# Attention scores of two directions, summed on VectorE before the product with the values, in a hybrid attention and expert block

## The chip, the cores and the metric

One core of one Trainium2 chip runs the kernel. The metric is the device time of one execution in microseconds (us). Engines: TensorE (PE: matmuls, and PEld, its weight loads), VectorE (DVE), ScalarE (ACT), GpSimd (POOL) and SyncE (SP, which here issues the large loads). Each engine runs its own instructions in order, and waits for another engine or a transfer at the places that the build has set.

## The reference, cut to what matters

One layer on 256 tokens of width 1024, with 256 context tokens ahead of them. A combined projection feeds two branches: a gated linear attention that runs over the tokens forward and backward (8 heads of 128, chunks of 64), and a chunk MLP. Both are projected, gated, added and projected again; a top-4-of-32 mixture of experts follows. The part that the change touches, for one direction:

```python
scores = jnp.einsum('bthd,bshd->bhts', qc * jnp.exp(b - b_ref), kc * jnp.exp(b_ref - b))
scores = jnp.where(lower, scores, 0.0)
o = (jnp.einsum('bhts,bshv->bthv', scores, vc)
     + jnp.einsum('bthd,bhdv->bthv', qc * jnp.exp(b), s))
...
o = (gla_chunked(q, k_f, i, logf_f, s_fwd0)
     + rev(gla_chunked(rev(q), rev(k_b), rev(i), rev(logf_b), s_bwd0)))
```

The output of a head is the sum of both directions, and the values (`i`) are the same in both.

## The kernel before

The kernel has a prefix (modulation, projection, attention, MLP branch, branch and output projections, router) and an expert part that streams the weights of 32 experts, 2 MB at a time, through a ring of buffers.

The projection's large products run as split fp32: `parts` (L316, through `split` at L258 and L259) writes a weight granule as a rounded `ghi` (on ACT, L258) and a rest `glo` (on DVE, L259), and `dense` (L325 to L340) makes three matmuls for each block, all recorded as L339. A granule of 256 columns is loaded by L311, 1 MB, on SP's queue.

Attention is done in pairs of heads, five turns `j` = 0 to 4. In turn `j` the projections of pair `j` (`d` steps) are written in between the steps of the two heads of pair `j`-1 (`x` and `y`: 0 `decays`, 1 `states`, 2 `output`, 3 `finish`) and two modulation steps (`m`), by a list written by hand:

```python
ORDER = "x0 d0 y0 m0 d1 x1 m1 d2 x2 y1 x3 m2 d3 y2 m3 y3 d4"
```

The four steps of a head:

- `decays` (L436 to L471): logarithms on ACT (L443), cumulative sums by scans on DVE (L450), differences `d1` (L459), exponentials on ACT (L462 to L466), products on DVE (L468 to L470). L469 and L470 end it; `e1`, `e2` lie in the tile `lf`.
- `states`: scores of both directions into PSUM (L487, 32 small matmuls), masked into one of two tiles `masked` (L490, named `attc` in the trace), keys transposed (L497) and copied (L498), outer products of keys and values (L506, L509).
- `output`: the chunk states are chained on DVE (L520, L521); then, into `o_ps`, scores times values (L525) and queries times states (L529).
- `finish`: the norm of the head. `rstd_of` is a chain of some twelve small DVE operations (L105 to L111, about 0.2 us apart), `on` scales (L543), PE transposes `on` (L546), `y` multiplies the gate in (L548), and a split writes it into `yhl`.

Behind the last turn come: the projection of `v` in four granules, each followed by `prefetch` (L623: the first three 2 MB pieces of expert 0, into buffers that lie where attention's tiles lay); the norm of `v` (L638 to L643); branch_a, four granules of `w_branch_a` times `yhl` (L339 `acc<-yhl`); then the MLP branch, where L657 multiplies `v` by a position matrix into `o_ps` and L660 evicts it. L684 is 8 small matmuls for the router's base.

The build decides the order of each engine's instructions: it schedules by its own estimate of times, and keeps the written order only in part. So an edit can move rows far from it. The expert part has an order written by hand.

Of the kernel before, what the change touches and what calls it, by code (L numbers as in the profile page):

```python
# [26 lines left out]
def view(t, off, dims):  # L27
    return bass.AP(tensor=t.tensor, offset=t.offset + off, ap=[t.ap[0], *dims])
# [3 lines left out]
def kernel(  # L32
# [5 lines left out]
    ve, sc, te, gp = nc.vector, nc.scalar, nc.tensor, nc.gpsimd  # L38
# [122 lines left out]
    for h in range(2):  # L161
        b = slice(h * 64, h * 64 + 64)
# [16 lines left out]
    def bank(name, shape=(P, 2, T)):  # L179
        return ps.tile(list(shape), F32, name=name, bufs=2 if name in ("acc", "tp") else 1)  # L180
# [141 lines left out]
    def win(sec, j, pieces=False):  # L322
        return Granule(w_in[0, :, sec * D + j * 256:sec * D + (j + 1) * 256], pieces)
# [23 lines left out]
    def four_outs(pps, natural):  # L347
        if natural:
# [9 lines left out]
    start = [(win(1, 0, True), True, [bank("acc"), bank("acc")]), (win(2, 0, True), False, [bank("ua"), bank("ub")]),  # L358
             (win(3, 0, True), False, [bank("scores"), bank("o_ps")])]
# [23 lines left out]
    for k in range(2):  # L383
        a, b = cols2[:, 8 + 16 * k:16 + 16 * k], cols2[:, 16 + 16 * k:24 + 16 * k]
# [51 lines left out]
    def decays(hd, k, q):  # L436


        col = slice(hd, hd + 1)
        lf = wk.tile([P, 2, 2 * T], F32, name="lf")  # L440
        tc.keep_in_program_order(sc.preload_act_table_set("natural_log_exp_and_others"))
        for dr in range(2):
            tc.keep_in_program_order(sc.activation(lf[:, dr], k[:, dr], AF.Ln, scale=omlb[dr][:, col], bias=lb[dr][:, col]))  # L443
        kl, kc = k[:, :, 0:T], k[:, :, T:2 * T]
        bl = wk.tile([P, 2, T], F32, name="bl")
        cu = wk.tile([P, 2, T], F32, name="cu")
        ve.memset(view(cu, T - 1, [[1, 2]]), 0.0)

        def scan(dst, o, src, so, m, n, st):
            ve.tensor_tensor_scan(view(dst, o, [[st, n]]), m, view(src, so, [[st, n]]), 0.0, op0=OP.mult, op1=OP.add)  # L450

        whole = view(reset, 1, [[0, T - 1]])
        scan(bl, 0, lf, 0, reset, T, 1)
        scan(bl, 2 * T - 1, lf, 3 * T - 1, reset, T, -1)
        scan(cu, T - 2, lf, 2 * T - 1, whole, T - 1, -1)
        scan(cu, T + 1, lf, 3 * T, whole, T - 1, 1)
        e1, e2 = lf[:, :, 0:T], lf[:, :, T:2 * T]
        d1 = wk.tile([P, 2, T], F32, name="d1")
        ve.tensor_sub(view(d1, 0, [[T, 2], [64, 4], [1, 64]]), view(bl, 0, [[T, 2], [64, 4], [1, 64]]),  # L459
                      view(bl, 31, [[T + 1, 2], [64, 4], [0, 64]]))  # L460
        w = wk.tile([P, 2, 2, 4], F32, name="w")
        sc.activation(e1, d1, AF.Exp)  # L462
        sc.activation(e2, d1, AF.Exp, scale=-1.0)
        sc.activation(cu, cu, AF.Exp)
        sc.activation(w[:, 0], view(bl, 31, [[T + 1, 2], [64, 4]]), AF.Exp)
        sc.activation(w[:, 1], view(d1, 63, [[T - 63, 2], [64, 4]]), AF.Exp)  # L466
        for dr in range(2):
            ve.scalar_tensor_tensor(e1[:, dr], e1[:, dr], nomlb[dr][:, col], q, op0=OP.mult, op1=OP.mult)  # L468
        ve.scalar_tensor_tensor(e2, kl, -1.0, e2, op0=OP.add, op1=OP.mult)  # L469
        ve.scalar_tensor_tensor(cu, kc, -1.0, cu, op0=OP.add, op1=OP.mult)  # L470
        return e1, e2, cu, w  # L471

    def attend(hd, dec, iv, og):

        hh = hd % 2
        vs = slice(hh * P, hh * P + P)
        st = {}

        def states():
            qt, kt_, kc, w = dec  # L480
            for dr in range(2):
                for tt in range(2):
                    for b in range(4):
                        t0, n = 64 * (b // 2), 64
                        if b % 2 != dr:
                            t0, n = t0 + 32 * (1 - dr), 32
                        te.matmul(pst[32 * b:32 * b + 32, dr, tt, t0:t0 + n], kt_[:, dr, tt * P + 32 * b:tt * P + 32 * b + 32],  # L487
                                  qt[:, dr, tt * P + t0:tt * P + t0 + n], start=True, stop=True, skip_group_check=True)
            sm = masked[hd % 2]
            ve.copy_predicated(sm, view(mask, 0, [[P, 2], [0, 2], [1, P]]), pst)  # L490
            ks = consts.tile([P, 2, 2, 4, P], F32, name="ks", tag="big3")
            kn, S = ks[:, 0], ks[:, 1]
            for a, src in ((0, kt_), (1, kc)):
                pt = bank("tp", (P, 2, 2, P))
                for dr in range(2):
                    for tt in range(2):
                        te.transpose(pt[:, dr, tt], src[:, dr, tt * P:tt * P + P], ident)  # L497
                nc.any.tensor_copy(kn[:, a], pt.rearrange("p a b c -> p (a b) c"))  # L498
            ua = bank("ua", (P, 4, P))
            ub = bank("ub", (P, 4, P))  # L500
            U = {}
            for slot, even, odd in ((0, (0, 0), (0, 1)), (1, (0, 2), (1, 1)), (2, (1, 2), (1, 3))):
                for bk, (dr, ch) in ((ua, even), (ub, odd)):
                    s = slice((ch % 2) * 64, (ch % 2) * 64 + 64)
                    U[dr, ch] = bk[:, slot]
                    te.matmul(bk[:, slot], kn[s, 0, 2 * dr + ch // 2], iv[s, ch // 2, vs], start=True, stop=True)  # L506
            for bk, dr in ((ua, 0), (ub, 1)):
                for tt in range(2):
                    te.matmul(bk[:, 3], kn[:, 1, 2 * dr + tt], iv[:, 2 + tt, vs], start=tt == 0, stop=tt == 1)  # L509
            st.update(sm=sm, S=S, R=kn, U=U, ua=ua, ub=ub)  # L510

        def output():
            qt, w = dec[0], dec[3]
            sm, S, R, U, ua, ub = (st[k] for k in ("sm", "S", "R", "U", "ua", "ub"))
            sc.activation(S[:, 0, 0], ua[:, 3], AF.Copy, scale=w[:, 0, 0, 0:1])
            sc.activation(S[:, 1, 3], ub[:, 3], AF.Copy, scale=w[:, 0, 1, 3:4])
            for n in range(3):
                for dr, a, b in ((0, n, n + 1), (1, 3 - n, 2 - n)):
                    r = R[:, dr, b]
                    ve.tensor_add(r, S[:, dr, a], U[dr, a])  # L520
                    ve.tensor_scalar(S[:, dr, b], r, w[:, 1, dr, a:a + 1], w[:, 0, dr, b:b + 1], op0=OP.mult, op1=OP.mult)  # L521
            o = bank("o_ps", (P, 2, P))
            for tt in range(2):
                for dr in range(2):
                    te.matmul(o[:, tt], sm[:, dr, tt], iv[:, tt, vs], start=dr == 0, stop=False, skip_group_check=True)  # L525
                for dr in range(2):
                    for cc in range(2):
                        ch = 2 * tt + cc
                        te.matmul(o[cc * 64:cc * 64 + 64, tt], qt[:, dr, ch * 64:ch * 64 + 64], S[:, dr, ch],  # L529
                                  start=False, stop=dr == 1, skip_group_check=True)  # L530
            st["o"] = o

        def finish():
            o = st["o"]
            ss = sm2.tile([P, 2], F32, name="ss")
            for tt in range(2):
                junk = mid.tile([P, P], F32, name="junk2")
                sc.activation(junk, o[:, tt], AF.Square, accum_out=ss[:, tt:tt + 1])
            rs = sm2.tile([P, 2], F32, name="rs")
            rstd_of(rs, ss, 1.0 / P, sm2)  # L540
            on = wk.tile([P, 2, P], F32, name="on")
            for tt in range(2):
                ve.tensor_scalar(on[:, tt], o[:, tt], rs[:, tt:tt + 1], None, op0=OP.mult)  # L543
            pt = bank("tp", (P, T))
            for tt in range(2):
                te.transpose(pt[:, tt * P:tt * P + P], on[:, tt], ident)  # L546
            y = wk.tile([P, T], F32, name="y")
            ve.scalar_tensor_tensor(y, pt, gncol, og[:, hh], op0=OP.mult, op1=OP.mult)  # L548
            split(y, yhi[:, hd], ylo[:, hd])
        return states, output, finish  # L550

    sc2 = late.tile([P, 8], F32, name="sc2")
# [4 lines left out]
    for j in range(5):  # L557
        if j < 4:
            iv = wk.tile([P, 4, 256], F32, name="iv")
# [8 lines left out]
        if prev:  # L568
            piv, pq, pog, psg = prev
            heads = []  # L570
            for hh in range(2):
                dec = []
# [61 lines left out]
    st = late.tile([P, 2, 2, 6], F32, name="st")  # L634
# [15 lines left out]
    for j in range(4):  # L650
# [4 lines left out]
        for gg in range(2):  # L655
            for n in range(2):
                te.matmul(pss[:, gg, n], v[:, n, (2 * j + gg) * P:(2 * j + gg + 1) * P], wsT[:, 2 * j + gg],  # L657
                          start=True, stop=True)
# [43 lines left out]
    for j in range(4):  # L702
# [29 lines left out]
        for k in range(2):  # L732
            kt = 2 * j + k
            for tt in range(2):
                te.matmul(pl[:, tt], h2[:, k, tt * P:(tt + 1) * P], wr_sb[:, kt], start=kt == 0 and tt == 0,
                          stop=kt == KT - 1, skip_group_check=True)
# [353 lines left out]
```

## Time and profile before

| | |
|---|---|
| median of 3 runs | 1410.64 us (1410.29 to 1414.01) |
| profiled execution, its own time | 1409.58 us |
| its span | 1407.8 us |
| PE busy | 1335.7 us (95%) |
| DVE busy | 598.0 us (42%) |
| ACT busy | 302.0 us (21%) |
| moved by DMA | 487.35 MB, mean 346 GB/s |
| mean granted clock of PE | 0.988 |

The busy shares are means over the whole span. The two parts of the program have different limits, so that a stretch has to be read with its own row: PE's busy time, and the rate of the DMA engines.

### The profile page before, as it was taken

Reading aid. Unit: us, or ns where it says so; the run is one execution under the profiler, and the core shown is the slowest. Engines: PE = TensorE matmul, PEld = TensorE weight load, DVE = VectorE, ACT = ScalarE, POOL = GpSimd, SP = SyncE. Lnnn points to the kernel's source line nnn. Section 1 sums busy time; section 2 is a strip of 40 time slices with the busy share of each in tenths; the row PEclk is TensorE's granted clock in tenths of the full one; section 3 lists DMA queues with packets and bytes.
Section 4 is the critical chain, followed back from the end, with each engine's and each line's share of the span. In section 5 each row is a group of like instructions: output and inputs, shape, how many; then the busy total and the mean of one; then the engine's idle time right before and its main releaser. Section 6 shows DMA issues by size and latency. Waiting matters only on the chain. (4 is left out here: it accounts for less than half of the span.)

```text
span 1407.8 us, 18376 instructions
## 1 busy us (share of the span) xinstructions
PE 1335.7 (95%) x7815; PEld 722.9 (51%) x7815; DVE 598.0 (42%) x1176; ACT 302.0 (21%) x496; POOL 57.8 (4%) x59
## 2 busy tenths in 40 slices
PE   6999999989999999999999998989999899898986
PEld 4897988879999533333333332323323233232322
DVE  5578868697578322322232232222222222222214
ACT  3373645544344110000010010100001000010001
POOL 3000000000055000000000000000000000000001
PEclk7999999999999999999999999999999999999999
DMA  9545445366677989999999999999999999999995
GB/s 334 184 156 194 136 165 180 118 212 258 222 232 251 412 350 428 427 426 428 426 428 427 425 429 426 427 426 427 427 427 426 428 427 427 428 425 427 427 425 200
DMA packets 101264, 487.35 MB, mean 346 GB/s; under 512 B 5653, under 2 KB 64154, under 8 KB 76474
## 3 DMA queue, kind: packets, MB, share of 16 engines
q1 hardware_dynamic: 100042, 482.85, 85.3%
q0 software_dynamic: 848, 2.75, 0.7%
q8 instruction: 63, 1.03, 0.3%
q10 hardware_dynamic: 288, 0.52, 0.1%
q14 instruction: 23, 0.19, 0.0%
HBM read 485.06 MB, written 1.05 MB: 345 GB/s over the span
## 5 line engine op out<-in xcount | busy, mean ns | idle before, releaser
L828 PE MATMUL gate<-w,xT 128*64 128x512 f32 x1024 | 271.2, 608 | 18.3 <-DMA w<-in_w_dram 17.2
L828 PE MATMUL lin<-w,xT 128*64 128x512 f32 x1024 | 263.9, 594 | 0.0
L865 PE MATMUL py<-w,hT 128*64 128x512 f32 x992 | 221.0, 594 | 18.0 <-DMA w<-in_w_dram 18.0
L884 DVE SCALAR_TENSOR_TENSOR acc<-sc,wts,acc 128x512 f32<-128x512 f32 x122 | 86.0, 746 | 208.9 <-PE sc L881 208.9
L828 PEld LDWEIGHTS lin<-w,xT 128*64 128x64 f32 x1024 | 73.5, 137 | 147.8 <-issue 147.8
L339 PE MATMUL acc<-hh,glo 128*128 128x256 f32 (+1 forms) x480 | 146.2, 305 | 2.5 <-DVE glo L259 2.5
L339 PE MATMUL acc<-hh,ghi 128*128 128x256 f32 (+1 forms) x480 | 147.5, 307 | 0.7 <-ACT iv L424 0.7
L865 PEld LDWEIGHTS py<-w,hT 128*64 128x64 f32 x992 | 70.1, 136 | 149.2 <-issue 114.1
L259 DVE TENSOR_TENSOR glo<-w,ghi 128x1024 fp32r<-128x1024 f32 (+1 forms) x99 | 125.6, 1276 | 48.9 <-ACT ghi L258 48.7
L339 PE MATMUL acc<-hl,ghi 128*128 128x256 f32 (+1 forms) x480 | 145.1, 302 | 0.0
L828 PEld LDWEIGHTS gate<-w,xT 128*64 128x64 f32 x1024 | 62.0, 136 | 159.6 <-issue 96.0
L258 ACT ACTIVATE ghi<-w 128x1024 fp32r<-128x1024 f32 (+1 forms) x102 | 101.4, 1009 | 141.7 <-PE acc L339 68.3
L868 DVE TENSOR_TENSOR y<-py,g2h 128x512 f32<-128x512 f32 x31 | 21.4, 692 | 177.9 <-PE py L865 177.9
L339 PEld LDWEIGHTS acc<-hh,glo 128*128 128x128 f32 x480 | 90.0, 188 | 8.3 <-DVE glo L259 3.7
L339 PEld LDWEIGHTS acc<-hh,ghi 128*128 128x128 f32 x480 | 90.3, 188 | 5.3 <-ACT iv L424 0.9
L339 PEld LDWEIGHTS acc<-hl,ghi 128*128 128x128 f32 x480 | 90.3, 188 | 3.8 <-issue 0.4
L803 ACT ACTIVATE xT<-misc,sh,a 128x128 f32<-128x128 f32 (+1 forms) x68 | 30.7, 451 | 282.1 <-DVE xT L805 282.1
L805 DVE TENSOR_SCALAR xT<-misc,a,sh 128x128 f32<-128x128 f32 (+1 forms) x68 | 27.2, 401 | 138.3 <-PE misc L799 127.8
L836 ACT ACTIVATE s<-g 128x512 f32<-128x512 f32 x32 | 20.2, 630 | 288.3 <-DVE g L835 288.3
L799 PEld LDWEIGHTS misc<-p,acc 128*128 128x128 f32 x544 | 67.4, 198 | 27.4 <-issue 26.0
L835 DVE TENSOR_SCALAR g<-gate 128x512 f32<-128x512 f32 x32 | 22.1, 692 | 134.7 <-PE gate L828 134.7
L799 PE MATMUL misc<-p,acc 128*128 128x128 f32 (+1 forms) x544 | 73.6, 289 | 0.9 <-DVE p L790 0.9
(316 smaller groups left out, 1476.8 us busy)
## 6 DMA issues: line engine op xcount, KB each, us to landing
w<-in_w_dram SPq DMA_DIRECT2D x187, 2048.0 KB, 37.7
w<-in_w_in_dram SPq DMA_DIRECT2D x33, 1024.0 KB, 8.2
w<-in_w_mod_dram SPq DMA_DIRECT2D x24, 1024.0 KB, 6.4
w<-in_w_dram SPq DMA_DIRECT2D x10, 1024.0 KB, 33.9
w<-in_w_branch_a_dram SPq DMA_DIRECT2D x4, 1024.0 KB, 5.2
w<-in_w_branch_b_dram SPq DMA_DIRECT2D x4, 1024.0 KB
w<-in_w_out_dram SPq DMA_DIRECT2D x4, 1024.0 KB
w<-in_w_in_dram SPq DMA_DIRECT2D x12, 256.0 KB, 9.4
```

Of the source, the lines that this page charges most:

```text
L258: sc.activation(hi, src, AF.Copy)
L259: eng.tensor_sub(lo, src, hi)
L339: te.matmul(o, l, r, start=opens and kt == 0 and n == 0, stop=kt == KT - 1 and n == 2, skip_group_check=True)
L799: te.matmul(pg[:, k], view(x1, tt * D + kt // 2 * 256 + kt % 2, [[2, P]]), tok[:, tt], start=tt == 0, stop=tt == 1)
L803: sc.activation(xT[:, kt], pg[:, k], AF.Identity, bias=sh2[:, kt:kt + 1], scale=a2[:, kt:kt + 1])
L805: ve.tensor_scalar(xT[:, kt], pg[:, k], a2[:, kt:kt + 1], sh2[:, kt:kt + 1], op0=OP.mult, op1=OP.add)
L828: te.matmul(zz[n][h * C:(h + 1) * C], xT[:, kt], w[:, 0, n * D + h * 512:n * D + (h + 1) * 512], start=False, stop=kt == KT - 1, skip_grou ...
L835: ve.tensor_scalar(g, zz[0], 7.0, None, op0=OP.min)
L836: sc.activation(s, g, AF.Sigmoid, scale=1.702)
L865: te.matmul(py[h * C:(h + 1) * C], hT2[:, kt % 4, (kt // 4) * C:(kt // 4) * C + C], w[:, k, h * 512:(h + 1) * 512], start=False, stop=kt = ...
L868: ve.tensor_mul(y, py, g2h)
L884: ve.scalar_tensor_tensor(acc[:, tt, s], pcs[h], wcol[tt], old[:, tt, s], op0=OP.mult, op1=OP.add)
```

## The change

`decays` also returns `d1`, which nothing reads after the exponentials. In `states`, the two masked score tiles of a head (one for each direction) are added on DVE into `d1`, seen as two tiles of 128 columns. In `output`, this sum is multiplied by the values once for each of the two token tiles, where there was one product for each direction. In all 16 fp32 matmuls of 128x128x128 go and 8 adds of 128x256 come.

```diff
-        return e1, e2, cu, w
+        return e1, e2, cu, w, d1
...
-            qt, kt_, kc, w = dec
+            qt, kt_, kc, w, d1 = dec
...
             ve.copy_predicated(sm, view(mask, 0, [[P, 2], [0, 2], [1, P]]), pst)
+            sums = d1[:, 0].rearrange("p (a b) -> p a b", a=2)
+            ve.tensor_add(sums, sm[:, 0], sm[:, 1])
...
-            st.update(sm=sm, S=S, R=kn, U=U, ua=ua, ub=ub)
+            st.update(sm=sums, S=S, R=kn, U=U, ua=ua, ub=ub)
...
             for tt in range(2):
-                for dr in range(2):
-                    te.matmul(o[:, tt], sm[:, dr, tt], iv[:, tt, vs], start=dr == 0, stop=False, skip_group_check=True)
+                te.matmul(o[:, tt], sm[:, tt], iv[:, tt, vs], start=True, stop=False, skip_group_check=True)
```

Lines behind the add have new numbers: two more up to the matmul (L487 stays, L497 is L499, L520 is L522), which is L526, and one more behind it (L543 is L544, L546 is L547, L623 is L624, L657 is L658, L684 is L685).

The build's order moves as well. Up to the output of the first head the engines' rows are the same; from there on they differ, up to the MLP branch. The expert part keeps its order. Three places:

SP, which issues the loads, at the end of attention: `w_in` are granules of the projection, `w_branch_a` those of the branch projection, `in_w` with 128x4096 the prefetches of expert 0.

```order
 L311 DMA w<-in_w_in_dram 128x8x256 x4
-L311 DMA w<-in_w_branch_a_dram 128x8x256 x4
-L623 DMA w<-in_w_dram 128x4096 x3
+L311 DMA w<-in_w_branch_a_dram 128x8x256
+L624 DMA w<-in_w_dram 128x4096 x3
+L311 DMA w<-in_w_branch_a_dram 128x8x256 x3
 L311 DMA w<-in_w_in_dram 128x8x256 x5
 L311 DMA w<-in_w_branch_b_dram 128x8x256
```

Three of the four `w_branch_a` loads now stand behind the prefetches, which wait for the `y` of head 7 and its split.

PE, in the branch projection. `acc<-yhl` are its dense matmuls, 48 for each of four granules. Before, at the end of the fourth granule:

```order
L339 MATMUL acc<-yhl,ghi 128x256 x2
L339 MATMUL acc<-yhl,glo 128x256
L657 MATMUL o_ps<-wsT,v 128x128 x4
L684 MATMUL ub<-wr_sb,sh_71 128x32 x8
L657 MATMUL o_ps<-wsT,v 128x128 x8
L339 MATMUL acc<-hh,ghi 128x256
```

Of the change, at the end of the first granule:

```order
L339 MATMUL acc<-yhl,ghi 128x256 x2
L339 MATMUL acc<-yhl,glo 128x256
L685 MATMUL ub<-wr_sb,sh_71 128x32 x8
L658 MATMUL o_ps<-wsT,v 128x128 x12
L339 MATMUL acc<-yhl,ghi 128x256 x2
```

The MLP branch's first matmuls and those of the router's base have moved from behind the fourth granule of branch_a to between its first and its second. The transposes of head 7 (L547), on which the prefetches hang, stand 86 dense matmuls ahead of the first granule; before it was 27 (L546).

PE in the last attention turn, at the scores of head 6. `on` is the scaled output of head 5. Before:

```order
L487 MATMUL scores<-lf 32x64
L497 MATMUL tp<-ident,lf 128x128 x4
L497 MATMUL tp<-ident,cu 128x128 x4
L339 MATMUL acc<-hh,ghi 128x256
L339 MATMUL acc<-hl,ghi 128x256
L525 MATMUL o_ps<-iv,attc 128x128 x2
```

Of the change:

```order
L487 MATMUL scores<-lf 32x64
L339 MATMUL acc<-hh,ghi 128x256
L339 MATMUL acc<-hl,ghi 128x256
L547 MATMUL tp<-ident,on 128x128
L499 MATMUL tp<-ident,lf 128x128 x4
L547 MATMUL tp<-ident,on 128x128
```

The transposes of head 5's output now stand among those of head 6's keys; before they stood some 100 rows ahead of the scores. On DVE the same head's `on` has moved behind both L469. Of the change, DVE:

```order
L459 TENSOR_TENSOR d_2919<-bl 128x512
L470 SCALAR_TENSOR_TENSOR cu<-sg_2185,cu 128x512
L110 SCALAR_TENSOR_TENSOR nt<-nt,nv 128x2
L468 SCALAR_TENSOR_TENSOR lf<-lf,lbn_720,q 128x256
L468 SCALAR_TENSOR_TENSOR lf<-lf,lbn_734,q 128x256
L469 SCALAR_TENSOR_TENSOR lf<-sg_2185,lf 128x2x256
L111 SCALAR_TENSOR_TENSOR rs<-nt,ny 128x2
L470 SCALAR_TENSOR_TENSOR cu<-sg_2186,cu 128x512
...
L469 SCALAR_TENSOR_TENSOR lf<-sg_2186,lf 128x2x256
L544 TENSOR_SCALAR on<-o_ps,rs 128x128 x2
```

Before, this chain of small rows and `on` (L543) stood wholly ahead of the scans of head 6's decays.

## Rows read from the trace of the kernel before

**Rows 1.** The page: engines' busy time, and the rate of transfers in 40 slices.
```profile
PE 1335.7 (95%) x7815; PEld 722.9 (51%) x7815; DVE 598.0 (42%) x1176; ACT 302.0 (21%) x496; POOL 57.8 (4%) x59
GB/s 334 184 156 194 136 165 180 118 212 258 222 232 251 412 350 428 427 426 428 426 428 427 425 429 426 427 426 427 427 427 426 428 427 427 428 425 427 427 425 200
```
**Rows 2.** Windows of 50 us; the head names the columns.
```profile
core 0: us, PE busy (x) PEld busy (x) DVE busy (x) ACT busy (x) POOL busy (x), PEclk, DMA share, GB/s
300.00:350.00 50.00, 49.56 (x427) 47.23 (x426) 40.91 (x95) 22.17 (x34) 0.00 (x0) 1.00 0.68 239
550.00:600.00 50.00, 50.00 (x246) 18.44 (x246) 15.21 (x28) 4.29 (x8) 0.00 (x0) 1.00 1.01 427
```
**Rows 3.** The instructions of L525: ns shortest/median/longest, first and last start.
```profile
L525 PE MATMUL o_ps<-iv,attc x64: 270/275/378, 114.2 to 320.3; 128*128 128x128 f32 x64
```
**Rows 4.** Timeline of PE, first and last head: start, us, instruction.
```profile
114.16 0.60 PE L525 MATMUL o_ps<-iv,attc 128*128 128x128 f32 x4
114.69 0.43 PE L529 MATMUL o_ps<-ks,lf 128*64 128x128 f32 x2
...
319.89 0.71 PE L525 MATMUL o_ps<-iv,attc 128*128 128x128 f32 x4
320.53 0.66 PE L529 MATMUL o_ps<-ks,lf 128*64 128x128 f32 x8
```
**Rows 5.** Groups by line, DVE from 95 to 335 us; the last is the page's.
```profile
L490 DVE COPY_PREDICATED attc<-attc,scores 128x512 f32<-128x512 int32 x8 | 5.9, 739 | 0.0
L110 DVE SCALAR_TENSOR_TENSOR nt<-nt,nv 128x2 f32<-128x2 f32 x24 | 3.8, 159 | 0.6
L259 DVE TENSOR_TENSOR yhl<-y,yhl 128x256 fp32r<-128x256 f32 x7 | 3.0, 422 | 1.2 <-ACT yhl L258 1.2
...
L258 ACT ACTIVATE ghi<-w 128x1024 fp32r<-128x1024 f32 (+1 forms) x102 | 101.4, 1009 | 141.7 <-PE acc L339 68.3
```
**Rows 6.** Waits of PE from 95 to 335 us: total, times, longest.
```profile
PE scores L487 <- DVE lf L469: 4.1, 1, 4.1
PE acc L339 <- DVE glo L259: 1.7, 4, 0.8
```
**Rows 7.** Timeline of ACT in the last attention turn.
```profile
276.37 0.21 ACT L465 ACTIVATE w<-bl 128x8 f32<-128x8 f32 x1 [1.37 <-DVE bl L450]
279.78 1.52 ACT L443 ACTIVATE lf<-sg,lba,lbb 128x512 f32<-128x512 f32 x2
```
**Rows 8.** Timeline of DVE, the end of the decays of heads 6 and 7.
```profile
284.96 0.69 DVE L469 SCALAR_TENSOR_TENSOR lf<-sg,lf 128x512 f32<-128x512 f32 x1
285.56 0.68 DVE L470 SCALAR_TENSOR_TENSOR cu<-sg,cu 128x512 f32<-128x512 f32 x1
...
286.95 0.69 DVE L469 SCALAR_TENSOR_TENSOR lf<-sg,lf 128x512 f32<-128x512 f32 x1
```
**Rows 9.** Timeline of PE: transposes in the turn before, scores in the last.
```profile
226.25 0.66 PE L497 MATMUL tp<-ident,lf 128*128 128x128 f32 x4
...
285.70 0.87 PE L487 MATMUL scores<-lf 128*32 128x64 f32 x32 [4.09 <-DVE lf L469]
286.50 1.12 PE L497 MATMUL tp<-ident,lf 128*128 128x128 f32 x4
```
**Rows 10.** Window of 5 us behind that wait (columns as in rows 2).
```profile
285.00:290.00 5.00, 4.30 (x77) 4.07 (x78) 5.00 (x9) 4.97 (x6) 0.00 (x0) 0.66 0.61 223
```
**Rows 11.** Timeline of SP's queue, 330 to 337 us.
```profile
330.54 5.20 SPq L311 DMA_DIRECT2D w<-in_w_branch_a_dram  x3
335.79 1.52 SPq L623 DMA_DIRECT2D w<-in_w_dram  x3
```
**Rows 12.** Windows of 5 us at the branch projection (columns as in rows 2).
```profile
325.00:330.00 5.00, 5.00 (x47) 5.00 (x46) 4.86 (x12) 2.25 (x3) 0.00 (x0) 1.00 0.00 0
335.00:340.00 5.00, 5.00 (x44) 5.00 (x44) 3.50 (x8) 2.62 (x3) 0.00 (x0) 1.00 1.09 348
350.00:355.00 5.00, 5.00 (x45) 5.00 (x44) 1.92 (x2) 1.05 (x1) 0.00 (x0) 1.00 1.04 439
```
**Rows 13.** The instructions on `yhl`, branch projection (columns as in rows 3).
```profile
L339 PE MATMUL acc<-yhl,ghi x128: 278/280/284, 335.8 to 358.2; 128*128 128x256 f32 x128
```
**Rows 14.** Timeline of PE behind the fourth granule.
```profile
358.39 1.05 PE L657 MATMUL o_ps<-wsT,v 128*128 128x128 f32 x8
...
362.90 1.16 PE L657 MATMUL o_ps<-wsT,v 128*128 128x128 f32 x8 [0.78 <-DVE t L660]
363.82 0.36 PE L339 MATMUL acc<-hh,ghi 128*128 128x256 f32 x1
```
**Rows 15.** DMA issues, 300 to 375 us: KB each, median us to landing.
```profile
w<-in_w_in_dram SPq DMA_DIRECT2D x8, 1024.0 KB, 13.5
w<-in_w_branch_a_dram SPq DMA_DIRECT2D x4, 1024.0 KB, 5.2
```
**Rows 16.** Timeline of DVE: the split of a half granule.
```profile
336.99 1.23 DVE L259 TENSOR_TENSOR glo<-w,ghi 128x1024 fp32r<-128x1024 f32 x1 [1.31 <-ACT ghi L258]
```

## The prediction

> **What bounds the kernel now.** I read the page first, then the trace in stretches, then the waits of TensorE (PE), then the single places that the new order touches. The page has PE busy for 1335.7 of 1407.8 us [rows 1], but that is an average over two parts. In stretches of 50 us the reader is to look at two columns together: from 300 to 350 us PE is busy for 49.56 of 50 us while the DMA engines move 239 GB/s; from 550 us on they move 427 GB/s, and the page shows about that figure in every slice to the end [rows 1, 2]. So the prefix (projection, attention, MLP branches, router; to about 480 us) is bound by PE, and the experts behind it by the transfer of their weights. The expert loads start only when the prefix gives them buffers; a microsecond off PE's path in the prefix moves the whole stream, and one put on it does too. VectorE (DVE) is far from full there: 40.91 of 50 us [rows 2]. PE waits for others in the attention stretch in one place above all: 4.1 us for L469, the last operation of the decays of head 6 [rows 6]. That is why the edit has to be read as three things: matmuls removed from the bound engine, adds put on an engine with room, and the rows that the build put elsewhere.
>
> **The 16 removed matmuls.** L525 stands in the trace with 64 records of 270 to 378 ns [rows 3]: 8 heads, 2 token tiles, 2 directions, and 2 records for each fp32 matmul. The record's length is not its price, since the records overlap. The price is the distance to what follows: four records start at 114.16 and the next group at 114.69, 0.53 us; at the other end of the attention part it is 319.89 to 320.53, 0.64 us [rows 4]. The change takes 32 records away. 32 x 0.53 / 4 = 4.2 us, 32 x 0.64 / 4 = 5.1 us. I take 4.3, near the first, because most heads stand like it between dense matmuls. A matmul that is spread between other work costs PE its full distance, so nothing hides this gain by itself.
> The Trainium skill ("FP8 and Floating Point Precision", TensorE Precision Notes) says that true fp32 takes four passes through the array. At the full clock that would be 4 x 128 columns at 2.4 GHz, 0.21 us a matmul and, as an estimate, 3.4 us for the 16; the rows show 0.27 us a matmul, and the sum goes by the rows.
>
> **The 8 added adds.** No row of before is this add. The nearest is the split of y, a two-operand operation of 128x256 fp32 on DVE: 422 ns [rows 5]. 8 x 0.42 = 3.4 us on DVE. The tile that it writes is dead after the exponentials, and its neighbours (lf, w) live as long as it will now, so I see no new wait for a buffer. The cover is the work that PE has between the scores of a head and its output: L526 stands behind the transposes, the outer products and dense matmuls in the new order, so I put 0. Without that cover each head would wait 0.42 us more, 3.4 us in all; that is the upper bound and a rival below. A gain is excluded, since DVE does more than before.
>
> **The last attention turn (heads 6 and 7).** Before, DVE ended head 5 (rs, on, y) and only then came to the decays of head 6; PE transposed `on` long before it waited. After, the small operations of head 5's rstd chain stand between the scans and products of head 6, `on` stands behind both L469, and PE's transpose L547 stands between head 6's scores and the transposes of its keys. Two things follow. First, ScalarE (ACT) had waited 1.37 us in front of L465, ahead of the table loads and the second Ln at 279.78 [rows 7]; in the new order L465 stands behind the Ln's, so the chain that ends in L469 at 284.96 [rows 8] can end up to 1.37 us earlier. Three rstd operations of 0.16 us each [rows 5], 0.2 with the gap, now stand in its last stretch, 0.6 us. So the wait of 4.09 us [rows 9] shrinks by 0.8, to 3.3. Second, PE reaches L547 some 0.8 us behind the start of the scores, and `on` comes after L111 (0.2), L470, two L468 and L469 (2.08 us from 285.56 to the end of the second L469 at 287.64 [rows 8]) and itself 0.3: about 2.5 us, less 0.8 leaves a wait of about 1.5 (1.7 by the plain difference; copies and dense work move it by some tenths). Net +0.7 us. Bounds: -1.4, if `on` is there in time; +2.3, if the first wait stays at 4.09 and the second is 1.7 and the slow clock behind them lasts longer. PE ran at a granted clock of 0.66 from 285 to 290, behind that wait [rows 10]: four transposes took 1.12 us there and 0.66 at 226.25 [rows 9].
> The turn before (heads 4 and 5) has the same pattern with L547 among the scores, but the dense matmuls behind it waited for weights in before already, so I put 0, up to +1.5.
>
> **The branch projection and the expert prefetch.** This is the term that I fear most. The three prefetches of expert 0 (6.3 MB) stood behind the last three loads of w_branch_a; now they stand ahead of them. Before, those loads were issued at 330.54 to 335.7 and the prefetches at 335.79 [rows 11], while the DMA engines moved nothing from 325 to 330 [rows 12]. Call t the start of the first branch_a granule on PE (335.8 in before [rows 13]). In the new order the prefetches wait for the y of head 7, whose transposes now stand 86 dense matmuls ahead of t. A granule is 48 such matmuls, and the 192 of branch_a run from 335.8 to 358.4, 5.65 us a granule [rows 13, 14]; so 86 are 10.1 us, and with the 0.5 us of y the first prefetch starts near t-9.5. What a load does behind the prefetches is shown in before by the w_in loads of that stretch, which stand behind them: 13.5 us to landing, against 5.2 for a branch_a load with nothing in front [rows 15]. With 0.43 MB/us [rows 2, 12], the 7.34 MB of the prefetches and the next branch_a load take 17.1 us. Of the 5.2 us a transfer of 1.05 MB is 2.4, so the rest is 2.8. The load lands at t - 9.5 + 17.1 + 2.8 = t+10.4, call it t+11; the split of its first half (ACT 1.0, DVE 1.23 [rows 5, 16]) is done by t+13.3. PE wants this granule at t+5.65. But L685 and L658 now stand right there, not after the last granule: 5.4 us of which 0.78 is a wait [rows 14]. So PE would be ready at t+11.05 with the same waits as before, and the weights hold it to t+13.3: +2.3 us. Bounds: 0, if the load lands by t+8.7; +5.7, if the queue runs at 348 GB/s, as from 335 to 340 [rows 12] (7.34 MB then take 21.1 us, landing at t+14.4).
>
> **Sum.** -4.3 + 0 + 0.7 + 0 + 2.3 = -1.3 us against the profiled execution of 1409.58 us: 1408.3. The median of the runs, 1410.64, is 1.06 above that execution, so the forecast is 1409.3 us.
>
> **The rivals.**
> Plain saving: the moved rows find cover, the load lands by t+8.7 and `on` is in time or its wait is paid back by the shorter first one. Then only the matmuls count, -4.3 to -5.1, in the middle -4.7: 1410.64 - 4.7, about 1405.9 us. For it: all the waits of PE in the attention stretch together are 7 us, so small ones are mostly covered. Against it: the w_in loads took 13.5 us behind the same prefetches.
> Slower: PE starves at the second branch_a granule. Place: PE between L658 and the second granule; price 5.7 us or more, and 1.3 for the slow clock that followed the one long wait in before. It decides once the load lands later than about t+16, where -4.3 + 0.7 + 7.6 passes +4.0; with 5.7 + 1.3 and the turn's upper bound 2.3 it is 1415.6. For it: nothing in the order protects the load. Against it: at 0.43 MB/us it lands 5 us sooner. The Trainium skill ("TensorE: Matmul & The Clock Gate", Why this matters for your kernels) asks for no idle gaps of PE between bursts; the rows at 285 us agree.
> The adds on the path: DVE delays the decays and L526 by 3.4 us in all: -1.3 + 3.4, 1412.7 us. Against it: L490, 0.74 us long [rows 5], stands at the same place, and no wait of PE behind it is in the list.
> No change reaches the end: the expert stream starts by something else than PE: 1410.6 us.
>
> **How the numbers follow.** Forecast 0.50, plain saving 0.25, starved granule 0.13, adds on the path 0.08, nothing 0.04. A difference within 0.3% (4.2 us) can't be told from none here: faster means under 1406.4, slower over 1414.9. Faster: two thirds of the plain saving and a tenth of the forecast, 0.22. Slower: most of the starved granule, 0.11. Same: 0.67. The range, 1405.0 to 1414.5, takes in the plain saving to -5.6 and leaves out the far half of the starved granule; the forecast alone has 1406.5 to 1412.5.
>
> **What would show it.** Right: L526 with 32 records and 0.13 us to the next row each; adds of 0.42 us; L469 ending a wait of about 3.3 us and `on` one of about 1.5 right behind; PE waiting about 2 us for w_branch_a's split between L658 and the second granule; the stream at 427 GB/s starting about 1.3 us earlier. Wrong: a wait of 4 us or more at that granule, a wait of L526 for the add, or new waits where the order of the first turns is unchanged.

## The result, and the profile after

The changed kernel takes 1418.87 us (median of 20 runs, 1412.36 to 1421.47) where the kernel before, run beside it, takes 1410.65 (20 runs, 1404.46 to 1416.94). The ratio is 1.0052, interval 1.004 to 1.0065: slower by 0.5%, 7.3 us by the ratio (the two medians are 8.2 apart). The forecast was 1409.3, its range ended at 1414.5, and the sign is the other one.

The profiled execution of the change took 1419.65 us, its span is 1417.9 us, 10.1 more than before. The page, engines' busy time:

```profile
PE 1340.3 (95%) x7783; PEld 724.4 (51%) x7783; DVE 600.6 (42%) x1184; ACT 301.6 (21%) x496; POOL 57.9 (4%) x59
```

Against [rows 1], PE has 32 instructions fewer and is busy 4.6 us longer: it did less in more time, part of it at a slower clock, as the stretches below show. The groups of the two edited lines (ns shortest/median/longest, first and last start):

```profile
L526 PE MATMUL o_ps<-iv,d x32: 270/275/378, 114.2 to 318.5; 128*128 128x128 f32 x32
...
L492 DVE TENSOR_TENSOR d<-attc x8: 406/414/432, 109.9 to 295.2; 128x256 f32<-128x256 f32 x8
```

The edit itself is as forecast: half of the records of [rows 3], and adds (L492) of 0.41 us each. The waits of PE from 95 to 335 us, and from 335 to 420:

```profile
PE acc L339 <- ACT ghi L258: 4.0, 2, 2.7
PE scores L487 <- DVE lf L469: 3.3, 1, 3.3
...
PE acc L339 <- ACT ghi L258: 2.1, 1, 2.1
PE o_ps L658 <- DVE t L661: 1.6, 2, 0.8
```

Against [rows 6] the wait for L469 is shorter, as forecast; new are the three waits for `ghi`, the rounded weights, one of 2.7 us in a turn of which the prediction says nothing. Every place can be read in the stretches of 5 us (columns as in [rows 2]):

```profile
165.00:170.00 5.00, 1.69 (x10) 1.48 (x11) 2.46 (x4) 3.53 (x4) 0.00 (x0) 0.96 0.43 158
170.00:175.00 5.00, 5.00 (x46) 4.64 (x44) 4.55 (x7) 3.33 (x5) 0.00 (x0) 0.70 0.01 2
285.00:290.00 5.00, 2.77 (x40) 2.40 (x40) 5.00 (x11) 4.92 (x7) 0.00 (x0) 0.57 0.53 196
290.00:295.00 5.00, 5.00 (x65) 4.37 (x65) 5.00 (x9) 1.49 (x3) 0.00 (x0) 0.75 0.00 0
350.00:355.00 5.00, 2.85 (x11) 2.56 (x12) 2.67 (x3) 3.06 (x3) 0.00 (x0) 0.55 0.91 291
355.00:360.00 5.00, 5.00 (x36) 5.00 (x35) 2.14 (x2) 1.06 (x1) 0.00 (x0) 0.77 0.01 4
```

Look at the second number (PE busy) and the granted clock (third from the end) together: at three places PE first stands, and then works at a lower clock. Before, the clock in these stretches was 1.00, but for the 0.66 of [rows 10].

**Place 1: the turn of heads 2 and 3, at 167 us.** The timeline of the change, all engines (start, us, instruction; in brackets the idle time before it and what ended it):

```profile
157.64 0.68 DVE L469 SCALAR_TENSOR_TENSOR lf<-sg,lf 128x512 f32<-128x512 f32 x1
158.24 0.60 DVE L544 TENSOR_SCALAR on<-o_ps,rs 128x128 f32<-128x128 f32 x2
158.76 1.21 DVE L259 TENSOR_TENSOR glo<-w,ghi 128x1024 fp32r<-128x1024 f32 x1
160.00 0.37 SPq L311 DMA_DIRECT2D w<-in_w_in_dram  x1
163.23 0.57 PE L487 MATMUL scores<-lf 128*32 128x64 f32 x32
166.45 2.96 ACT L258 ACTIVATE ghi<-w 128x1024 fp32r<-128x1024 f32 x3 [3.64 <-DMA w<-in_w_in_dram]
167.56 0.39 PE L339 MATMUL acc<-hh,ghi 128*128 128x256 f32 x1 [2.74 <-ACT ghi L258]
168.82 0.38 PE L339 MATMUL acc<-hh,glo 128*128 128x256 f32 x1 [0.75 <-DVE glo L259]
169.49 0.30 PE L339 MATMUL acc<-hl,ghi 128*128 128x256 f32 x1
169.60 0.40 PE L339 MATMUL acc<-hh,glo 128*128 128x256 f32 x1
169.81 0.42 PE L339 MATMUL acc<-hh,ghi 128*128 128x256 f32 x1
...
174.56 0.71 PE L511 MATMUL ua<-iv,ks 128*128 128x128 f32 x4
```

and the same place of the kernel before:

```profile
158.36 1.22 DVE L259 TENSOR_TENSOR glo<-w,ghi 128x1024 fp32r<-128x1024 f32 x1
159.60 0.37 SPq L311 DMA_DIRECT2D w<-in_w_in_dram  x1
160.80 0.68 DVE L469 SCALAR_TENSOR_TENSOR lf<-sg,lf 128x512 f32<-128x512 f32 x1
164.64 0.57 PE L487 MATMUL scores<-lf 128*32 128x64 f32 x32
164.66 2.01 ACT L258 ACTIVATE ghi<-w 128x1024 fp32r<-128x1024 f32 x2 [4.39 <-DMA w<-in_w_in_dram]
167.03 0.39 PE L339 MATMUL acc<-hh,glo 128*128 128x256 f32 x1 [0.56 <-DVE glo L259]
...
171.24 0.49 PE L509 MATMUL ua<-iv,ks 128*128 128x128 f32 x2
```

It is a chain of four engines. DVE's split of one half granule (L259) reads the buffer that SP's next load wants; that load starts as soon as the split has ended, ACT rounds it, and PE multiplies by it. Before, the split stood ahead of L469 on DVE; now L469 and `on` stand in front of it. Measured from PE's scores, the split starts 4.47 us ahead (163.23 less 158.76) instead of 6.28, and the load takes 6.45 us from issue to ACT instead of 5.06: 1.8 us of the delay are the split's and 1.4 the load's. So PE, which came 1.41 us earlier (163.23 against 164.64; 1.1 of it are the four matmuls that two heads have less, 2 x 0.53), stands for 2.74 and 0.75 us. Then its records, 0.11 us apart up to 169.60, are 0.21 apart: the lower of its two levels. The full outer products behind it (L509 before, L511 now) start at 174.56 instead of 171.24, so that 1.41 us ahead has become 3.32 behind: the place costs 4.7 us. (A small part of it is moved work: 12 small matmuls of the next head's scores, 0.3 us, now stand ahead of L511.)

**Place 2: the last turn, heads 6 and 7.** The timeline, PE and ACT:

```profile
285.21 1.28 ACT L567 ACT_TABLE_LOAD   x1
285.97 0.87 PE L487 MATMUL scores<-lf 128*32 128x64 f32 x32 [3.28 <-DVE lf L469]
286.51 0.60 ACT L567 ACTIVATE mb<-acc 128x512 f32<-128x512 f32 x1
287.00 2.94 ACT L258 ACTIVATE ghi<-w 128x1024 fp32r<-128x1024 f32 x3
288.11 0.58 PE L339 MATMUL acc<-hh,ghi 128*128 128x256 f32 x1 [1.26 <-ACT ghi L258]
288.70 0.41 PE L547 MATMUL tp<-ident,on 128*128 128x128 f32 x1
```

The first wait is 3.28 us against 4.09 in [rows 9]. A second one follows, but not for `on`: PE waits 1.26 us for rounded weights, since ACT has a table load and L567 ahead of them; by 288.70 `on` is there. The clock stays low until past 290. Ahead of the first wait the change was 1.08 us behind (282.69 against 281.61, the starts less the waits); at the first branch granule it is 1.41 behind (337.18 against 335.77), though two more heads had saved 1.1 on the way. So the turn costs 1.4 us: 0.4 are waits (4.54 against 4.09), and 1.0 is the longer slow stretch (busy time times what is missing of the clock: 2.4 against 1.5, an estimate).

**Place 3: the branch projection.** The timeline, SP, ACT and PE:

```profile
328.51 2.48 SPq L624 DMA_DIRECT2D w<-in_w_dram  x3
331.19 16.50 SPq L311 DMA_DIRECT2D w<-in_w_branch_a_dram  x3
...
337.18 0.40 PE L339 MATMUL acc<-yhl,ghi 128*128 128x256 f32 x2
...
342.84 1.87 PE L685 MATMUL ub<-wr_sb,sh 128*128 128x32 f32 x16
346.46 1.16 PE L658 MATMUL o_ps<-wsT,v 128*128 128x128 f32 x8 [0.78 <-DVE t L661]
348.40 1.16 PE L658 MATMUL o_ps<-wsT,v 128*128 128x128 f32 x8 [0.78 <-DVE t L661]
350.58 2.00 ACT L258 ACTIVATE ghi<-w 128x1024 fp32r<-128x1024 f32 x2 [12.60 <-DMA w<-in_w_branch_a_dram]
351.68 0.80 PE L339 MATMUL acc<-yhl,ghi 128*128 128x256 f32 x2 [2.12 <-ACT ghi L258]
352.94 0.58 PE L339 MATMUL acc<-yhl,glo 128*128 128x256 f32 x1 [0.46 <-DVE glo L259]
...
371.60 0.28 PE L339 MATMUL acc<-hh,ghi 128*128 128x256 f32 x1
```

The first granule starts at 337.18 (call it t again). The first matmul behind branch_a and L658 starts 34.4 us later; before it was 28.0 ([rows 13, 14]: 335.8 to 363.82). The place costs 6.4 us. At 363.82 before and 371.60 now the change is 7.8 us behind, which is all that the ratio shows; the span's other 2.3 us lie behind that point, within the spread of single executions.

### The profile page after: what moved, and what is told of

The parts are those of the page before. It is cut to its first block, busy times and chain, and to the rows that moved or that the text cites. A ratio compares the mean times of both kernels' runs of the same rounds, so it can differ in the third digit from the quotient of the medians.

```text
span 1417.9 us, 18319 instructions
## 1 busy us (share of the span) xinstructions
PE 1340.3 (95%) x7783; PEld 724.4 (51%) x7783; DVE 600.6 (42%) x1184; ACT 301.6 (21%) x496; POOL 57.9 (4%) x59
## 5 line engine op out<-in xcount | busy, mean ns | idle before, releaser
L259 DVE TENSOR_TENSOR glo<-w,ghi 128x1024 fp32r<-128x1024 f32 (+1 forms) x99 | 126.3, 1283 | 56.5 <-ACT ghi L258 56.4
L339 PEld LDWEIGHTS acc<-hh,ghi 128*128 128x128 f32 x480 | 91.1, 190 | 10.1 <-ACT ghi L258 4.7
```

Of the source, the lines that this page charges most:

```text
L259: eng.tensor_sub(lo, src, hi)
L339: te.matmul(o, l, r, start=opens and kt == 0 and n == 0, stop=kt == KT - 1 and n == 2, skip_group_check=True)
```

## The experiments

An edit makes the build decide the whole order anew. To price the edit and the order apart, the kernels here hold every engine's order of the prefix by a list: each instruction gets an edge to the one ahead of it in the list, which orders and waits for nothing else. The two copies that the build may put on any engine stay where they were; the expert part is left to its own order.

```diff
+    for n in order:
+        i = ins[int(n)]
+        e = str(i.engine)
+        if e in prev:
+            tc.add_manual_dep(i, prev[e].name, mybir.DependencyInfo(mybir.DependencyClass.NoSync, mybir.DependencyReason.DATA), reason="order")
+        prev[e] = i
```

"Old order" is that of the kernel before with each add put behind its L490; "new order" that of the changed kernel. Ratios are to the kernel before on the same chip (1411.69, 1411.5 and 1411.88 us in the three groups of runs).

**Control: the kernel before, held by the list.** The edit is the list alone.

> A control: the kernel before with nothing changed but that its own order is held by the explicit list that the other runs use. If the list is neutral: within 0.1 or 0.2% of before, 1410 to 1413 us. If the list itself gains or costs, the other runs have to be read against this one.

1412.38 us, ratio 1.0002 (0.9989 to 1.0015). Holding the order costs nothing that can be measured.

**The edit in the old order.** The diff of the change, with the old order's list:

```diff
+        pin(tc, nc, OLD_ORDER)
```

> The whole edit (8 adds, 16 matmuls fewer), but every engine's rows are held in the order of the kernel before by an explicit list; each add stands right behind its L490. Order theory (the edit itself saves, the moved rows lose): 1410.7 - 4.3, about 1406.4 us; no wait of PE at the second branch_a granule, the wait for L469 again near 4.1 us, no ACT wait near 167 us. Edit theory (the add delays DVE's splits and scans, or the longer life of d1 costs): still 1417 to 1419 us, as the change.

1409.0 us, ratio 0.998 (0.9964 to 0.9997). The sign turns: the edit is not what makes the kernel slower. But the gain is smaller than 4.3. Timelines of this kernel, place 1 (this execution is 1.8 us early already at the first scores, 96.0 against 97.8, so only distances within it are read):

```profile
156.22 1.22 DVE L259 TENSOR_TENSOR glo<-w,ghi 128x1024 fp32r<-128x1024 f32 x1
157.47 0.37 SPq L311 DMA_DIRECT2D w<-in_w_in_dram  x1
162.38 0.57 PE L487 MATMUL scores<-lf 128*32 128x64 f32 x32
165.01 0.38 PE L339 MATMUL acc<-hh,glo 128*128 128x256 f32 x1 [0.76 <-DVE glo L259]
```

The split is 6.16 us ahead of the scores, as before, and only a short wait is left. The waits of PE from 95 to 335 us sum to 10.0 us against 7.2 before. The largest part of the difference is a wait for L523, the chaining of the states (1.6 against 0.4), where the add now stands ahead of it on DVE; the rest lies at small places, where weights and values (L259, L424) that were in time before are now wanted earlier.

**Before's operations in the new order.**

```diff
+        pin(tc, nc, NEW_ORDER)   # two L525 for each L526, no add
```

> The operations of the kernel before (two products for each token tile, no add), held in the order of the change. Order theory: the change's 1418.9 plus the 4.3 us of matmuls, about 1423 us, with the waits of the change at 167, 286 and 350 us. Edit theory: about 1410.7 us, as before, since nothing of the edit is in it.

1424.47 us, ratio 1.0106 (1.0082 to 1.013). PE waits 3.25 us for `ghi` at place 1, 3.22 for L469 and 1.57 for `ghi` at place 2, and twice 0.78, 1.89 and 0.47 at place 3: all of the new stalls, without the edit. The order makes them.

**New order up to the branch projection, old order from there.** On SP, and L685 and L658 on PE accordingly, with the rows of DVE and ACT that belong to them:

```diff
-L311 DMA w<-in_w_branch_a_dram 128x8x256
+L311 DMA w<-in_w_branch_a_dram 128x8x256 x4
 L624 DMA w<-in_w_dram 128x4096 x3
-L311 DMA w<-in_w_branch_a_dram 128x8x256 x3
```

> The whole edit; the order of the change up to the branch projection, that of before from there on (SP: the three branch_a loads ahead of the prefetches again; PE: L658 and L685 behind the fourth granule). Order theory: what the change loses at the branch projection, 6.5 us by the two traces, comes back: about 1412.4 us; the wait near 167 us stays. Edit theory: no difference from the change, 1418.9 us. If the loss lies in the attention turns alone, also 1418.9.

1414.86 us, ratio 1.0024 (1.0011 to 1.0038): no wait is left at place 3; at place 1 PE waits 3.35 and 0.71 us, at place 2 2.96 and 1.57. So attention's order alone costs 5.9 us over the edit in the old order (1409.0), and the branch's 4.0 more (1418.87 less 1414.86).

**Old order up to there, new order from there.** The same edit with + and - exchanged, in the old order.

> The whole edit; the order of before up to the branch projection, that of the change from there on. Order theory: attention saves its 4.3 us, but the prefetches now wait for a y of head 7 that comes 59 dense matmuls (7 us) later against the branch projection than in the change, so the branch_a load behind them lands some 7 us later and PE starves there for 9 us or more, with a slow clock behind it: 1410.7 - 4.3 + 9 + 3, about 1418 us. If the queue doesn't hold the load (it overtakes the prefetches): about 1407 us.

1422.72 us, ratio 1.0082 (1.0061 to 1.0104). At the second granule, PE:

```profile
357.12 0.80 PE L339 MATMUL acc<-yhl,ghi 128*128 128x256 f32 x2 [8.27 <-ACT ghi L258]
```

Here the prefetches start only at 334.0, 2.5 us ahead of t (336.5) and not 8.7, because head 7's transposes stand where they did before. The later the prefetches, the later the load behind them: 8.27 us instead of 2.12. The two halves of the order lean on each other. The place takes 13.0 us longer than before (336.47 to 377.52). Of the 4.7 us over the 1418 expected, 2.6 are the edit's (1409.0 in the old order, where 1406.4 was put in), and 1.0 is the place (13.0, where 9 and 3 were).

**Only the loads behind the prefetches, rest old order.** On SP the edit of the kernel above, on PE none.

> The whole edit in the order of before, but SP's three branch_a loads stand behind the three prefetches, as in the change; nothing else is moved. Queue theory (a load waits for all that stands ahead of it): the first prefetch starts near t-2.5 (t: first branch_a granule on PE), the load lands 19.9 us later (7.34 MB at 0.43 MB/us, and 2.8) at t+17.4, its first half is split by t+19.7, and PE, which wants it at t+5.65, waits 14 us with a slow clock behind: 1409.0 + 14 + 2, about 1425 us. Rival (it is the rows L658 and L685 between the granules that cost in the change, not the loads): 1409 us.

1426.41 us, ratio 1.0107 (1.0092 to 1.0121). SP and PE:

```profile
332.64 3.27 SPq L624 DMA_DIRECT2D w<-in_w_dram  x3
336.01 10.53 SPq L311 DMA_DIRECT2D w<-in_w_branch_a_dram  x2
...
354.95 0.80 PE L339 MATMUL acc<-yhl,ghi 128*128 128x256 f32 x2 [14.01 <-ACT v L632]
```

The trace names L632, which runs at 354.31 on ACT; but the row ahead of it there waited 19.61 us for the load of `w_branch_a`. The expected 14 us are there. That L685 and L658 were moved to this very place hides part of such a wait: it is 14.01 us here, and 8.27 with them in the kernel ahead.

**Only L685 and L658 moved, loads in the old order.** On DVE and ACT the rows that belong to them move too.

```diff
 L339 MATMUL acc<-yhl,glo 128x256
+L685 MATMUL ub<-wr_sb,sh_71 128x32 x8
+L658 MATMUL o_ps<-wsT,v 128x128 x12
 L339 MATMUL acc<-yhl,ghi 128x256 x2
...
-L658 MATMUL o_ps<-wsT,v 128x128 x4
-L685 MATMUL ub<-wr_sb,sh_71 128x32 x8
-L658 MATMUL o_ps<-wsT,v 128x128 x8
```

> The whole edit in the order of before on SP throughout and on all engines up to the branch projection; from there PE, VectorE and ScalarE have the rows of the change (L685 and L658 behind the first granule, with their evictions). Queue theory: the loads land in time, so only one more wait of 0.8 us for the eviction of o_ps comes: 1409.0 + 0.8, about 1410 us. Rival (the moved rows cost, by the norm of v that L658 waits for): some 4 us, 1413 us.

1412.07 us, ratio 1.0009 (0.9996 to 1.0023), between the two times that were expected, and 3.1 over the edit in the old order. The trace shows a second wait of 0.78 us for L661 (before, L684 stood between the L657 and covered one), and the place takes 1.0 us longer (337.9 to 366.95, against 333.2 to 361.27). The other 2 us lie where the order of the two kernels is the same: this execution is 2.4 us later already at the first scores (98.4 against 96.0), and from there to the branch PE waits 1.0 us more and has a stretch at a clock of 0.67 (305 to 310, behind a wait of 1.6 for L523) that the other execution hasn't. So the rows that moved are shown to cost 1.0; the rest is likely the spread of single executions.

**New order, one row back.** On DVE, place 1:

```diff
 L111 SCALAR_TENSOR_TENSOR rs<-nt,ny 128x2
+L259 TENSOR_TENSOR glo<-w,ghi 128x1024
 L468 SCALAR_TENSOR_TENSOR lf<-lf,lbn_720,q 128x256
...
 L544 TENSOR_SCALAR on<-o_ps,rs 128x128 x2
-L259 TENSOR_TENSOR glo<-w,ghi 128x1024
```

> The change as it is, but one row of VectorE is moved: the split (L259) that stood behind L469 and `on` at 158.76 us now stands six rows earlier, behind the rstd chain. Release theory (that split ends late, so its buffer comes free late, SP issues the next w_in load at 160.0, and PE waits 2.7 + 0.75 us for it at 167 us, with a slow clock from 169.6 to about 174): the load goes out some 2.5 us earlier, the wait and the slow clock go: 1418.9 - 4.8, about 1414 us. Rival (the load is late for another reason, the transfer itself or the queue): the wait stays, 1418.9 us.

1413.89 us, ratio 1.0016 (1.0003 to 1.0029): one row of 1.2 us gives back 5.0 of the 7.3. The stretch behind it, to be held against that of the change:

```profile
165.00:170.00 5.00, 5.00 (x58) 4.66 (x57) 5.00 (x9) 4.21 (x6) 0.00 (x0) 1.00 0.01 3
```

PE doesn't wait there, and the clock is the full one, 1.00 from 170 to 175 too.

**Both places mended.** This row, and the old order at the branch.

> The order of the change with both mends: the split of the second turn six rows earlier on VectorE, and the order of before from the branch projection on. If the two places make up the loss: 1418.9 - 5.0 (split early) - 4.0 (old branch), about 1410 us, near the whole edit in the order of before (1409.0). If the rest of the new order costs too: over 1412 us.

1408.15 us, ratio 0.9979 (0.9961 to 0.9997). With places 1 and 3 gone the sign turns, and the new order can't be told from the old one (1409.0, the intervals overlap almost wholly). Place 2 is still in it: PE waits 2.99 and 1.46 us there, and at the first branch granule this execution is 2.8 us ahead of before (333.00 against 335.77, from equal first scores at 97.8), near the 4.3 of the matmuls less the 1.4 of place 2. The branch's order is worth 5.7 us between this kernel and the one ahead of it, 4.0 in the pair above, and 6.4 in the trace of the change.

**The matmuls alone, old order.** The kernel leaves out the product of the backward direction's scores and the values, and has no add.

```diff
-                for dr in range(2):
+                for dr in range(1):
```

> Leaves out the backward direction's product of scores and values, and has no add: 16 matmuls fewer in the order of before, and nothing else. In that order the whole edit gave 1409.0 against 1411.7 in the same call, 2.7 us, where the matmuls are worth 4.3. Add theory (the adds on VectorE make PE wait 1.6 us longer): 1411.7 - 4.3, about 1407 us here. Rival (PE runs ahead of loads and splits that don't become faster, so part of any gain turns into waits): the same 2.7 us, 1409 us.

1410.29 us, ratio 0.9989 (0.998 to 0.9998): 1.6 us, at most 2.8. So 4.3 us of PE's work go, and under 3 arrive, with no add in the program. Its trace shows where some of it stays: PE's waits from 95 to 335 us sum to 8.4 us against 7.2, and the slow stretch behind the wait for L469 is longer (0.50 from 285 to 290 and 0.92 to 295, where before had 0.66 and 1.00), by busy time some 1.2 us (an estimate).

**The adds alone, old order.** The add's result isn't read, L525 stays.

> The order of before with the 8 adds on VectorE put in (their result isn't used) and both products kept. Cover theory: VectorE has room, 0 to +0.5 us. Rival (the adds lie on the path): up to +3.4 us, 1415 us. The run with the matmuls alone gained 1.2 us, the whole edit 2.7, so a cost of the adds isn't expected.

1412.47 us, ratio 1.0001 (0.9985 to 1.0017). The adds, 0.425 us each in its trace, cost nothing that the time shows, as forecast; the interval allows 2.4 us. The trace is less clean: PE waits 1.7 us for L523, behind one of the adds on DVE, against 0.7 in the control.

**Two rows by hand, in the old order with the edit.** On ACT, L465 of the last turn behind the Ln's (the forecast's 1.37 us); on DVE, one L523 ahead of L490.

```diff
-L465 ACTIVATE w<-bl 128x8
 L567 ACT_TABLE_LOAD
...
 L443 ACTIVATE lf<-sg_2186,lba_723,lbb_724 128x512
+L465 ACTIVATE w<-bl 128x8
```

> The whole edit in the order of before, and two rows moved: on ScalarE L465 of head 6, which waited 1.72 us in front of two table loads, stands behind the logarithms of head 7; on VectorE an L523 on which PE waited 1.58 us stands ahead of the mask and the add of head 7. Wait theory: the wait for L469 shrinks by 0.8 to 1.7 us, that for L523 by 1.2: 1409.0 - 2 to 3, 1406 to 1407 us, under before by 0.3% or more. Rival (as with the matmuls, what PE gains there it waits elsewhere): 1409 us.

1408.97 us, ratio 0.9982 (0.9965 to 1.0). The wait for L469 falls to 2.7 us, and a wait of 2.0 for `ghi` appears: no gain over the edit alone, as the rival had it. Of the versions tried, this, the edit in the old order and the one with both places mended have the lowest times, 0.2% under before (their intervals end at 1.0, 0.9997 and 0.9997), and can't be told apart.

## Why the prediction was wrong, step by step

**The step that failed most: the other turns, put at nothing.** The prediction gave the last turn +0.7, the turn ahead of it 0, and the others nothing at all. The turn of heads 2 and 3 cost 4.7 us in the trace; moving one row back returned 5.0. The mechanism is shown from both sides: the old operations in the new order have the stall, the new ones in the old order don't, and one split decides. The prediction went by the waits that the profile of before shows, and of this place [rows 6] hold only one of the short ones for `glo`, 0.56 us, since the chain from split to load to rounding ended just in time: ACT's first half was done by 165.7 (164.66 + 1.0), and PE came to it at 166.0. 0.3 us of slack is in no list of waits, and the new order of this turn, with the split behind L469 and `on`, is not among the places that the prediction weighs. The load's share of the delay, 1.4 us, couldn't be read from the order at all. The sentence "new waits where the order of the first turns is unchanged" asked only for turns whose order was the same; this one's had changed.

**The branch term: right mechanism, wrong size.** Forecast +2.3 (0 to 5.7), measured 6.4. By parts: the wait itself is 2.12 + 0.46 = 2.6, near the forecast's 2.3; but both sides of it came later than I put them. PE was ready at t+12.4 (348.40 + 1.16), not t+11.05, since L685 now stands ahead of the three L658 groups and covers no wait of them: a second 0.78, and 0.5 in ends of records, which overlap the next ones where PE doesn't stand. The load landed at t+13.4, not t+11: the first prefetch started at t-8.7 and not t-9.5, and SP could issue the second and third only behind the split of `y`, so the DMA engines moved 104 GB/s from 328 to 331; from 343 to 352 they moved 366 to 349, where the forecast had 430 throughout. And 2.4 us are clock: 2.85 us of work at 0.55 and 5.00 at 0.77 lose, worked out as busy time by what is missing of the clock, 1.3 and 1.2. 2.6 + 1.3 + 2.4 is 6.3 of the 6.4. That price stood in the rival ("1.3 for the slow clock") and not in the term.

**The matmuls, -4.3.** The records are gone, and PE's path is shorter by what was said where nothing else is due: at 163 us, behind two heads' outputs, the change is 1.41 ahead. The clause "so nothing hides this gain by itself" is what failed: a PE that is earlier meets weights that are not. The edit with the order held gives 2.8 (0.4 to 5.1, from its ratio), the matmuls alone 1.6 (0.3 to 2.8). In the trace of the matmuls alone, waits take 1.2 us of it and a longer slow stretch about as much; which small wait takes each tenth wasn't taken apart.

**The adds, 0.** Right for the change: 8 x 0.41 us, no wait of L526, and no difference of time when they stand alone (at most 2.4 us). The rival with 3.4 us is out. That they are hidden everywhere isn't shown: in the old order a wait for L523 grows behind them, from 0.7 to 1.7 us.

**The last turn, +0.7.** The first wait was right (3.3 forecast, 3.28 measured); the second was 1.26 us where 1.5 was forecast, but for another reason, ACT's order. The turn cost 1.4: the clock stayed low into a second stretch, 0.75 from 290 to 295, which only the bound of +2.3 had taken in.

**The sum again, with what was measured:** -4.3 + 4.7 + 1.4 + 6.4 = 8.2 in the trace, for 7.8 at 371.60; 0.35 of the difference is what the change was ahead at 163 us beyond the two heads' matmuls (1.41 less 1.06). Each of these is a difference of two single executions; kernels with the same order up to the branch took 236.9 to 239.5 us from the first scores to it, so it is the runs that bear out the 4.7 (5.0 came back) and the 6.4 (4.0 to 5.7 came back); the 1.4 rests on its own waits and clock alone. The plain saving (1405.9) fell with the order; the starved granule (1415.6) had one place right, but not its condition: the load landed at t+13.4, not past t+16, and the wait was 2.6 and not 5.7. "No change reaches the end" is out: the loss went through to the last instruction.

## What to carry to other kernels

Where a build decides the order, an edit of a few us is two experiments: the edit with the order held, and the order without the edit; here they were worth -3 and, by the ratios (1.0052 less 0.998, and 1.0106), +10 to +15 us. In a forecast, follow each row that sets a buffer free for a load (the split, then the load, the rounding, the product) through the whole new order, above all where the profile shows no wait: a place that was just in time is where a moved row costs most. And price a stall of the bound engine with the slow stretch behind it.

## What the runs showed of the hardware

PE's granted clock fell behind short stalls. Behind waits of 2.74 and 0.75 us it was 0.70 in the next stretch, with records 0.21 us apart instead of 0.11, the lower of its two levels (1.2 and 2.4 GHz); behind 3.28 and 1.26 it was 0.57 and then 0.75; behind 0.78, 0.78, 2.12 and 0.46 it was 0.55 and 0.77. The same rows at place 3 with the two waits of 0.78 us alone (the kernel with L685 and L658 moved) ran at 1.00. It isn't the length of a wait alone: behind one wait of 1.6 us for L523 the clock was 0.67 in that kernel and 1.00 in the edit in the old order. By busy time, each of the three stalls cost an estimated 0.4 to 0.6 of its length once more: 1.5 us (5.00 x 0.30) on 3.5, 2.4 on 4.5 (2.77 x 0.43 + 5.00 x 0.25), 2.4 on 4.1. Before, the single wait of 4.09 cost 1.5 (4.30 x 0.34). The Trainium skill ("TensorE: Matmul & The Clock Gate", Why this matters for your kernels) asks for no idle gaps between bursts of matmuls; these rows agree, and give the price here.

The load at place 1 took 6.45 us from issue to ACT in the change, 6.96 in the old operations with the new order (159.99 to 166.95) and 7.06 in the new order with the old branch, against 5.06 before, with the same load issued 0.4 us behind it in each. The trace has a likely cause. A transfer of 16 KB on the queue whose kind the profile gives as instruction ran near it. Its line for 157 to 168 us (packets, MB, share of the time of 16 engines), before and in the change:

```profile
q8 instruction: 1, 0.02, 0.6%
q8 instruction: 1, 0.02, 1.2%
```

In these three kernels that transfer ran 1.0 to 3.3 us behind the issue of the load, where the load's own data began to move; in the other eleven it came 5.2 us behind it or later, and the load took 4.99 to 5.24 us. No run moves that transfer by itself, so the cause is likely and not shown. In the kernel with the split one row back the load took 5.23, so its gain holds both parts.
